# A decoder block on one core: new places for the last gate tiles, two steps of the weight preparation moved, and the start of the attention stage reordered

## The chip, the core and the metric

The kernel runs on one core of a Trainium2 chip. A core has a matrix engine (TensorE, PE in the profile, with its weight loads as PEld), a vector engine (VectorE, DVE), an activation engine (ScalarE, ACT), a general engine (GpSimd, POOL) and an engine that only issues transfers here (SyncE, SP). Each works through its own list of instructions in order and waits on semaphores of the others. Sixteen DMA engines carry the transfers. The metric is the device time of one execution in microseconds (us), the median of several runs.

## The reference

One layer: a wide projection, three groups of dilated sliding-window attention joined by a softmax over the groups' denominators, a gated linear recurrence, two gated merges, an output projection and a layer norm. Sequence 2048, width 1024, 24 heads of 64 (three groups of eight), all float32.

```python
proj = x @ w_in[l] + b_in[l]
q, k, v, g_attn, u_lru, g_lru, gate_logits = jnp.split(proj, SPLIT_POINTS, axis=-1)
q, k = rope(q), rope(k)
for g, (window, dilation) in enumerate(((128, 1), (512, 4), (2048, 16))):
    o_g, lse_g = dilated_band_attention(q[:, :, g], k[:, :, g], v[:, :, g], window, dilation)
wts = softmax(stack(lses));  attn = sum(wts * outs) * silu(g_attn)
y_a = attn @ w_attn_proj[l]
u = causal_depthwise_conv(u_lru, conv_w[l], conv_b[l])
h = rg_lru(u, ...)
y_b = (h * silu(g_lru)) @ w_lru_proj[l]
gates = sigmoid(gate_logits)
out = (gates[0] * y_a + gates[1] * y_b) @ w_out[l] + b_out[l]
x = layer_norm(DEEPNORM_ALPHA * x + out, ln_gain[l], ln_bias[l])
```

## The kernel before

A float32 product is done as three products of rounded parts: each operand is split into a high part (a copy in the format fp32r) and a low part (what is left), and high x high, high x low and low x high are added up in PSUM.

**Stage A, the projection (0 to about 1447 us).** The 72 column tiles of `w_in` are taken in pairs, and the sequence in two halves of two chunks of 512. A pair in a half is a *position*; there are 36 in each half. Except for the first position of each half, a position's 2x2x2 block products are done as seven (Winograd's form of Strassen's method) instead of eight: the weights of a pair are four blocks A11, A12, A21, A22, and the sums are S1 = A21 + A22, S2 = S1 + A11, S3 = A21 + A11 and, here, S4 = S2 + A12. One product is a *tick*: 12 matmuls of 128x512, some 2.7 us. The order of the seven in a position is nearly always MID (1, 6, 7, 5, 2, 4, 3), which uses A11, S2, S3, S1, A12, A22, S4; the last position of a half has EDGE (1, 2, 6, 7, 4, 5, 3), the second position of a half FIRST.

A planner written out in Python sets the order of all engines. It walks through the ticks; at each it writes down the tick's product on PE, then the steps due at that tick (`at(tick, step)`), then steps of longer chains (rotary embedding, the recurrence, stores) as budgets of busy time per engine and free slots allow, and last the step that brings the product out of its PSUM bank (`evacuate`). There are four such banks, so a bank has to be free again four products later. With `t0` four ticks before a position's first product (three in the second half), the position's weights come as follows:

- `load_w` (L225) issues a load of a 128x512 block on SP. In the first half S1 and S3 start as loads of A21 at `t0 - 6`, and GpSimd adds A22 and A11 to them by DMA (`added`, L235) at `t0 - 4`; A11 is loaded at `t0 - 4`, A22 and A12, in that order, at `t0 - 3`. In the second half the low parts come back from DRAM, and A21, A22, A11, A12 are loaded.
- `sums` (L241) at `t0 - 1` forms S2 and then S4 (in the second half S1 before them, and S4 on GpSimd). `sum3` at `t0` forms S3 in the second half.
- `prep_w` (L262) at `t0 + j` splits the j-th block of the order: ScalarE rounds the high part (L266), VectorE takes the low part (helper `tt`, L221).

All tiles of 2 KB a partition in this stage lie in 32 slots; `take` hands out the slot that has been free longest, `give` puts it back. Results of a position are tiles named y. The last two pairs of the sequence are merge gates: each y is put through tanh on ScalarE (L381) and stored into `mg_scr`; from the last position on (`now["n"] >= base[NQ - 1]`), ScalarE issues that store itself (L383).

**Stage B, attention (to about 1665 us).** Its tiles take the same memory as the slots of stage A, and a write waits until the old tile's last reader is done. There are 48 rounds, four for each of 12 units (a group's pair of heads). Round i computes, for four blocks of 128 queries and two heads:

- `scores(i)` on PE into four PSUM banks (tag s); `peak` on VectorE adds the mask and takes the row's extreme (L1007, writes a p tile; eight p tiles rotate); `expo` on ScalarE exponentiates (L1015).
- For round i - 1: `turn` transposes the p tiles on PE into banks of tag t; `bring` copies them to ptb, four copies a round, on ScalarE (L1038) or VectorE (L1040). The third copy goes to VectorE when `light` holds, in every third round and in units of the third group.
- `values(i - 2)` on PE (L1053) into a further bank of tag t, four banks in all for `turn` and `values`; `leave(i - 3)` on VectorE copies that bank out (L1062 and on).

In each round the order is scores(i), leave(i - 3), the exponentials left over, then peaks, transposes, copies and exponentials in turn, and values(i - 2) at the end. Loads of later units and of v go two a round on SP.

**Stage C (to the end)** does the two branch projections, the merge, the output projection and the layer norm, PE being busy throughout.

Of the kernel before, what the change touches and what calls it, by code (L numbers as in the profile page):

```python
# [8 lines left out]
F32 = mybir.dt.float32  # L9
F32R = mybir.dt.float32r  # L10
AF = mybir.ActivationFunctionType
ALU = mybir.AluOpType
# [19 lines left out]
def hybrid_block_kernel(ctx: ExitStack, tc: tile.TileContext, a: dict, out: bass.AP):  # L32
    nc = tc.nc
    sp, act, dve, pool, pe = nc.sync, nc.scalar, nc.vector, nc.gpsimd, nc.tensor
# [56 lines left out]
    now = {"n": 0}  # L91
# [33 lines left out]
    sl_p = stA.enter_context(tc.tile_pool(name="sl_p", bufs=1))  # L125
    ps = stA.enter_context(tc.tile_pool(name="ps", bufs=2, space=PSUM))
    NS, NL = 32, 4
    TRACE = False
    vacant = list(range(NS))
    home = {}  # L130

    def take(name, dt=F32R):
        if not vacant:
            raise RuntimeError(f"no slot at {now['n']}: {[x[1].name if hasattr(x[1],'name') else x[1] for x in home.values()]} chains {len(chains)}")
        i = vacant.pop(0)
        t = sl_p.tile([P, CH], dt, tag=f"s{i}", name=name)
        home[id(t)] = (i, t)
        return t
# [32 lines left out]
    def spend(**eng):  # L171
        for k, v in eng.items():
            if k == "DVE" and now["n"] < base[len(seq)] - 6:
                v *= ALONE
            left[k] = left.get(k, 0.0) - v
# [44 lines left out]
    def tt(eng, out, in0, in1, op):  # L220
        eng.tensor_tensor(out=out, in0=in0, in1=in1, op=op)  # L221


    U, LO, raw = {}, {}, {}

    def load_w(s, n):
        r = raw[s, n] = take(f"w{n}_{s}", F32)
        sp.dma_start(r.rearrange("p (k f) -> p k f", f=P), w_part(s, "A21" if n[0] == "S" else n))

    def w_part(s, n):  # L230

        f = plan[s][1][int(n[1]) - 1][0]
        k = 4 * (int(n[2]) - 1)
        return a["w_in"][f, :, k:k + 4, :]

    def added(s, n, x):

        t = raw[s, n].rearrange("p (k f) -> p k f", f=P)
        pool.dma_start(t, w_part(s, x), accum_op=ALU.add)  # L239

    def sums(s):  # L241
        def add(n, x, y):
            t = raw[s, n] = take(f"{n}_{s}", F32)
            tt(pool if plan[s][0] and n == "S4" else dve, t, raw[s, x], raw[s, y], ALU.add)
        if plan[s][0]:
            add("S1", "A21", "A22")
            spend(DVE=.9)
        add("S2", "S1", "A11")
        add("S4", "S2", "A12")
        if plan[s][0]:  # L250
            spend(DVE=.9, POOL=1.4)
        else:
            spend(DVE=1.45)

    def sum3(s):

        t = raw[s, "S3"] = raw.pop((s, "A21"))
        tt(dve, t, t, raw[s, "A11"], ALU.add)
        spend(DVE=.9)
# [285 lines left out]
    light = [("v", FT_V + 2 * j, FT_V + 2 * j + 1) for j in range(6)]  # L545
# [6 lines left out]
    plan = []  # L552
# [3 lines left out]
    NQ = len(plan)  # L556
    ticks = [8 if pl[2] is None else 7 for pl in plan]
    base = [sum(ticks[:s]) for s in range(NQ + 1)]
# [116 lines left out]
    def at(t, fn):  # L675
        events.setdefault(t, []).append(fn)

    for s in range(1, NQ):
        t0 = base[s] - (3 if plan[s][0] else 4)
        if plan[s][2] is None:  # L680
            for d, n in ((4, "A21"), (4, "A11"), (3, "A22"), (3, "A12")):
                at(t0 - d, lambda s=s, n=n: load_w(s, n))
            for j in range(4):
                at(t0 + j, lambda s=s, j=j: prep_w(s, j))
            continue
        if plan[s][0]:
            for d, n in ((4, "A21"), (4, "A22"), (3, "A11"), (3, "A12")):
                at(t0 - d, lambda s=s, n=n: load_w(s, n))
        else:
            for d, n in ((6, "S1"), (6, "S3"), (4, "A11"), (3, "A22"), (3, "A12")):  # L690
                at(t0 - d, lambda s=s, n=n: load_w(s, n))
            for n, x in (("S1", "A22"), ("S3", "A11")):
                at(max(t0 - 4, 2), lambda s=s, n=n, x=x: added(s, n, x))
        at(max(t0 - 1, 4), lambda s=s: sums(s))
        if plan[s][0]:
            at(t0, lambda s=s: sum3(s))
        for j in range(7):
            if plan[s][0] and j % 2 == 0:
                at(t0 + j - 1, lambda s=s, j=j: load_lo(s, j))
            at(t0 + j, lambda s=s, j=j: prep_w(s, j))  # L700
    for s, pl in enumerate(plan):
        if pl[4] == "ug" and not (pl[0] and pl[1][1][0] - FT_U in put_off):
            at(base[s] + 1, lambda i=pl[1][1][0] - FT_U: fetch_gr(i))
        if pl[0] and pl[4] == "ug":
            i = pl[1][1][0] - FT_U
# [78 lines left out]
    def unit(u):  # L784

        return (0, 2, 1)[u % 3], u // 3
# [135 lines left out]
    for T, (s, j) in enumerate(where):  # L922
# [14 lines left out]
        low = min(low, len(vacant))  # L937
        if TRACE:
            print(T, s, j, plan[s][4], len(vacant), len(lo_vacant), len(chains), {k: round(v, 1) for k, v in left.items()})
    n = len(where)  # L940
# [101 lines left out]
    def values(i):  # L1042
        u, q = divmod(i, 4)
        g, hp = unit(u)
        V = VT[g, hp // 2]
        o = st["o", i] = aps.tile([P, 4, P], F32, tag="t", name=f"o{i}", bufs=4)
        for j in range(4):
            ptb = st["b", i, j // 2]
            n = 4 * q + j
            for x in range(first(i, j) // P, 2):  # L1050
                for h, hs in enumerate(HALF):
                    v0 = P * (hp % 2) + 64 * h
                    pe.matmul(o[hs, j, :], V[:, n if x else prev(g, n), v0:v0 + 64], ptb[:, j % 2, x, h, :],  # L1053
                              start=(x == first(i, j) // P), stop=(x == 1))

    def leave(i):
        u, q = divmod(i, 4)
        g, hp = unit(u)
        o, t = st.pop(("o", i)), ot[u]
        cs = slice(q * CH, (q + 1) * CH)  # L1060
        if g == 0:
            dve.tensor_copy(t[:, cs].rearrange("p (b q) -> p b q", b=4), o)  # L1062
        elif g == 1:
            dve.tensor_copy(t[:, cs].rearrange("p (j r) -> p j r", r=4), o.rearrange("p r j -> p j r"))
        else:
            dve.tensor_copy(t.rearrange("p (j r) -> p j r", r=16)[:, :, 4 * q:4 * q + 4], o.rearrange("p r j -> p j r"))
        if g < 2:
            later(1, lambda: sp.dma_start(o_scr[g][hp][:, cs], t[:, cs]))
        elif q == 3:
            later(1, lambda: sp.dma_start(o_scr[g][hp], t))  # L1070
        if q == 3:
            f0 = 4 * (3 * hp + g)
            dst = st_scr[:, f0:f0 + 4]
            if g == 0:
                later(1, lambda: sp.dma_start(dst.rearrange("(n q) f -> q n f", q=P), sta[u]))
            elif g == 2:
                later(1, lambda: sp.dma_start(dst.rearrange("(q n) f -> q n f", q=P), sta[u]))
            else:
                for c in range(4):
                    later(1, lambda c=c: sp.dma_start(dst[c * CH:(c + 1) * CH].rearrange("(q r) f -> q r f", r=4),  # L1080
                                                      sta[u][:, 4 * c:4 * c + 4]))
# [28 lines left out]
    NG = 48  # L1110
# [4 lines left out]
    for i in range(NG + 3):  # L1115
        u = i // 4
        on, turns = i < NG, 0 < i <= NG
        run(late)
        if i in VORD:
            loads += v_parts(*VORD[i])  # L1120
        if i % 4 == 0 and 1 <= u <= 9:
            loads += unit_parts(u + 2)
        for _ in range(2):
            if loads:
                loads.pop(0)()
        if on:
            scores(i)
        if i > 2:
            leave(i - 3)
        if turns:  # L1130
            expo(i - 1, 2, 1)
            expo(i - 1, 3, 0)
            expo(i - 1, 3, 1)
        if on:
            peak(i, 0, 0)
            expo(i, 0, 0)
            for j, h in ((0, 1), (1, 0), (1, 1)):
                peak(i, j, h)
        if turns:
            turn(i - 1, 0)  # L1140
            bring(i - 1, 0, 0, act)
            bring(i - 1, 0, 1, dve)
        if on:
            for j, h in ((0, 1), (1, 0), (1, 1)):
                expo(i, j, h)
            peak(i, 2, 0)
            peak(i, 2, 1)
        if turns:
            turn(i - 1, 1)
            light = unit((i - 1) // 4)[0] == 2 or i % 3 == 0  # L1150
            bring(i - 1, 1, 0, dve if light else act)
        if on:
            peak(i, 3, 0)
            peak(i, 3, 1)
            expo(i, 2, 0)
        if turns:
            bring(i - 1, 1, 1, dve)
        if i > 1 and i - 2 < NG:
            values(i - 2)
        if i in (40, 41):  # L1160
            prep_wl(i - 40, 2)
        if 42 <= i < 46:
            load_h(0, 2 * (i - 42), 2)
            load_h(0, 2 * (i - 42) + 1, 2)
        if i in (46, 47):
            prep_wl(i - 44, 2)
        now["n"] += 1
# [153 lines left out]
    for n in range(32):  # L1321
        c, f = divmod(n, 8)
# [223 lines left out]
```

## Time and profile before

| | |
|---|---|
| median of 3 runs | 2130.67 us (2128.5, 2130.67, 2130.9) |
| the profiled execution | 2126.78 us, of which the span from first to last instruction 2125.1 us |
| granted TensorE clock, mean over the span | 0.997 |
| DMA | 524.69 MB, mean 247 GB/s |
| chain that ended last, largest lines | PE q L619 43%, ACT p L1015 4%, PE yb L1300 to L1302 3% each |

How to read the rows that follow: a row of a timeline has the start in us, the duration, the engine and line, the operation, what it writes and reads, how many were merged, and in brackets the idle time of the engine before it and what ended that. A "q" behind an engine's name (SPq, ACTq, POOLq) is its sequencer, which issues transfers. A row of the waits has the engine, what it waited for, us in total, how many times, and the longest. Ends of matmuls are modelled.

### The profile page before, as it was taken

To read this page: it belongs to the slowest core of one execution; us is meant where nothing else is said; L and a number is where in the kernel's file an instruction comes from. 1 tells how busy PE (TensorE), PEld (TensorE's weight loads), DVE (VectorE), ACT (ScalarE), POOL (GpSimd) and SP (SyncE) were. 2 spreads that over 40 slices of the span, in tenths; PEclk is the share of its full clock that TensorE was granted. 3 is DMA by queue.
4 is the path that set the end of the run, shared out by engine and by line. 5 is a ranking of instruction groups with operands and counts; after the bars stand their busy time and mean duration, and the time that the engine had idled before them with its cause. 6 is when DMAs were issued, how large, how long until landed. Compare 5 with 4: busy or idle time off the path is not lost.

```text
span 2125.1 us, 35856 instructions
## 1 busy us (share of the span) xinstructions
PE 2084.5 (98%) x12016; PEld 1724.3 (81%) x12016; DVE 1668.6 (79%) x3193; ACT 1124.1 (53%) x2348; POOL 492.1 (23%) x465
## 2 busy tenths in 40 slices
PE   8999999999999999999999999998999999999998
PEld 7888888888888888888887887887888888888887
DVE  8878788899898877787787888776999645576667
ACT  6356455357356565656657666666999411121100
POOL 1111111111111002231131231224435434332120
PEclk9999999999999999999999999999999999999999
DMA  8987997988997976687788788779898788974431
GB/s 276 274 259 228 281 274 215 279 273 243 286 289 229 316 225 194 212 251 208 233 262 267 261 253 257 256 239 391 262 309 255 219 279 285 297 245 155 163 109 70
DMA packets 345832, 524.69 MB, mean 247 GB/s; under 512 B 124208, under 2 KB 153904, under 8 KB 341808
## 3 DMA queue, kind: packets, MB, share of 16 engines
q1 hardware_dynamic: 325760, 489.54, 71.3%
q0 software_dynamic: 12256, 19.42, 5.6%
q10 hardware_dynamic: 7632, 13.44, 1.8%
q8 instruction: 96, 1.57, 0.3%
q14 instruction: 88, 0.72, 0.1%
HBM read 317.14 MB, written 190.45 MB: 239 GB/s over the span
## 4 chain that ended last, share of the span: by engine, by line
PE 68%; ACT 5%; DVE 4%; DMA 2%; issue 1%; SPq 0%; DVEq 0%; ACTq 0%
PE q L619 43%; ACT p L1015 4%; PE yb L1300 3%; PE yb L1301 3%; PE z L1411 3%; PE yb L1302 3%; PE z L1410 3%; PE z L1412 3%; PE o L1053 2%; PE ya L1379 1%; PE ya L1378 1%; PE ya L1380 1%; PE g L489 1%; PE s L1000 1%; ACT ptb L1038 1%
## 5 line engine op out<-in xcount | busy, mean ns | idle before, releaser
L619 PE MATMUL q<-xT,hS 128*128 128x512 f32 x1680 | 520.8, 391 | 0.0
L619 PE MATMUL q<-xT,l 128*128 128x512 f32 x1120 | 436.0, 389 | 0.0
L619 PE MATMUL q<-xB,hA 128*128 128x512 f32 x1248 | 388.3, 392 | 5.6 <-ACT xB L209 5.6
L619 PEld LDWEIGHTS q<-xT,hS 128*128 128x128 f32 x1680 | 313.0, 188 | 69.0 <-issue 5.5
L619 PE MATMUL q<-xB,l 128*128 128x512 f32 x904 | 352.8, 390 | 0.1
L619 PEld LDWEIGHTS q<-xB,hA 128*128 128x128 f32 x1248 | 233.3, 188 | 57.4 <-ACT xB L209 5.6
L619 PEld LDWEIGHTS q<-xT,l 128*128 128x128 f32 x1120 | 210.2, 188 | 44.2
L619 PEld LDWEIGHTS q<-xB,l 128*128 128x128 f32 x904 | 170.0, 188 | 36.6 <-DVE l L221 0.9
L1015 ACT ACTIVATE p<-p,sta 128x256 f32<-128x256 f32 (+1 forms) x384 | 172.1, 455 | 11.7 <-DVE sta L1007 10.9
L239 POOL DMA_DIRECT2D wS<-in_w_in_dram x70 | 61.8, 955 | 502.9 <-DMA wS<-in_w_in_dram 117.3
L619 PE MATMUL q<-xB,hS 128*128 128x512 f32 x560 | 174.2, 392 | 2.4 <-DVE v L221 2.4
L619 PE MATMUL q<-xT,hA 128*128 128x512 f32 x560 | 173.0, 390 | 0.1
L266 ACT ACTIVATE hA<-wA 128x512 fp32r<-128x512 f32 x218 | 135.1, 624 | 64.3 <-DMA wA<-in_w_in_dram 25.9
L266 ACT ACTIVATE hS<-S 128x512 fp32r<-128x512 f32 x175 | 109.0, 623 | 85.0 <-DVE S L221 46.6
L221 POOL TENSOR_TENSOR S<-S,wA 128x512 f32<-128x512 f32 x35 | 45.5, 1300 | 423.1 <-DVE S L221 256.3
L1007 DVE CUSTOM_DVE_ANT_0 p<-s,mask 128x256 f32<-128x256 f32 (+1 forms) x384 | 118.9, 360 | 11.6 <-DMA mg_scr<-y 7.2
L619 PEld LDWEIGHTS q<-xB,hS 128*128 128x128 f32 x560 | 103.8, 188 | 25.4 <-issue 4.6
L619 PEld LDWEIGHTS q<-xT,hA 128*128 128x128 f32 x560 | 104.7, 188 | 23.4 <-issue 2.0
L221 DVE TENSOR_TENSOR l<-wA,hA 128x512 fp32r<-128x512 f32 x113 | 79.4, 703 | 27.8 <-ACT hA L266 27.6
L1411 PE MATMUL z<-wo,mh 128*128 128x512 f32 (+1 forms) x264 | 101.0, 383 | 0.0
L1412 PE MATMUL z<-wo,ml 128*128 128x512 f32 (+1 forms) x264 | 101.0, 383 | 0.0
L1410 PE MATMUL z<-wo,mh 128*128 128x512 f32 (+1 forms) x264 | 101.0, 383 | 0.0
(201 smaller groups left out, 4234.6 us busy)
## 6 DMA issues: line engine op xcount, KB each, us to landing
wA<-in_w_in_dram SPq DMA_DIRECT2D x253, 256.0 KB, 4.8
wl_scr<-l SPq DMA_DIRECT2D x105, 512.0 KB, 4.8
l<-wl_scr SPq DMA_DIRECT2D x105, 512.0 KB, 4.6
sw<-y SPq DMA_DIRECT2D x384, 64.0 KB, 3.2
wS<-in_w_in_dram SPq DMA_DIRECT2D x70, 256.0 KB, 4.8
wS<-in_w_in_dram POOLq DMA_DIRECT2D x70, 256.0 KB, 6.1
qh_scr<-hi SPq DMA_DIRECT2D x48, 256.0 KB, 5.4
v_scr<-vs SPq DMA_DIRECT2D x48, 256.0 KB, 4.5
```

Of the source, the lines that this page charges most:

```text
L221: eng.tensor_tensor(out=out, in0=in0, in1=in1, op=op)
L239: pool.dma_start(t, w_part(s, x), accum_op=ALU.add)
L266: act.activation(h, r, AF.Copy)
L619: pe.matmul(bank, w[:, ks], x[:, kk, xx], start=(first and i == 0), stop=(last and i == 11))
L1007: dve.tensor_tensor_reduce(out=st["p", i, j][:, h, lo:256], in0=st["s", i, j // 2][h][:, j % 2, lo:256], in1=mask[:, lo:256], scale=1.0, s ...
L1015: act.activation(p, p, AF.Exp, scale=-1.0, bias=s[:, h:h + 1], accum_out=s[:, 2 + h:3 + h])
L1300: pe.matmul(yb, WL[f][:, 0, k], xx[:, 0], start=(k == 0), stop=False)
L1301: pe.matmul(yb, WL[f][:, 0, k], xx[:, 1], start=False, stop=False)
L1302: pe.matmul(yb, WL[f][:, 1, k], xx[:, 0], start=False, stop=(k == 7))
L1410: pe.matmul(z, mh[:, k], w[:, 0, hs], start=(k == 0), stop=False)
L1411: pe.matmul(z, mh[:, k], w[:, 1, hs], start=False, stop=False)
L1412: pe.matmul(z, ml[:, k], w[:, 0, hs], start=False, stop=(k == 7))
```

## The change

Four parts. The last position's y tiles are put into chosen slots (31, 7, 8, 9, 30 as long as they are free) instead of the one free longest. S4 is formed by a step of its own, a tick later than S2. In the first half A12 is loaded ahead of A22, and A22 at a tick that depends on where product 4 stands in the order: a tick behind `t0` in MID instead of three ticks ahead of it, at `t0` in EDGE. At the start of stage B, values(0) comes behind scores(3), its copy-out `leave(0)` at the end of round 3, and the third copy of rounds 1 and 2 goes to VectorE.

```diff
+    LATE = [31, 7, 8, 9, 30]
...
     def take(name, dt=F32R):
...
-        i = vacant.pop(0)
+        i = vacant[0]
+        if name[0] == "y" and now["n"] >= base[NQ - 1]:
+            i = next((x for x in LATE if x in vacant), i)
+            if i in LATE:
+                LATE.remove(i)
+        vacant.remove(i)
...
+    def add_w(s, n, x, y):
+        t = raw[s, n] = take(f"{n}_{s}", F32)
+        on_pool = plan[s][0] and n == "S4"
+        tt(pool if on_pool else dve, t, raw[s, x], raw[s, y], ALU.add)
+        spend(**({"POOL": 1.4} if on_pool else {"DVE": .9 if plan[s][0] else .72}))
+
     def sums(s):
-        def add(n, x, y):
-            t = raw[s, n] = take(f"{n}_{s}", F32)
-            tt(pool if plan[s][0] and n == "S4" else dve, t, raw[s, x], raw[s, y], ALU.add)
         if plan[s][0]:
-            add("S1", "A21", "A22")
-            spend(DVE=.9)
-        add("S2", "S1", "A11")
-        add("S4", "S2", "A12")
-        if plan[s][0]:
-            spend(DVE=.9, POOL=1.4)
-        else:
-            spend(DVE=1.45)
+            add_w(s, "S1", "A21", "A22")
+        add_w(s, "S2", "S1", "A11")
...
-            for d, n in ((6, "S1"), (6, "S3"), (4, "A11"), (3, "A22"), (3, "A12")):
+            d22 = 3 if s == 1 else 4 - plan[s][2].index(4)
+            for d, n in ((6, "S1"), (6, "S3"), (4, "A11"), (3, "A12"), (d22, "A22")):
                 at(t0 - d, lambda s=s, n=n: load_w(s, n))
...
         at(max(t0 - 1, 4), lambda s=s: sums(s))
+        at(max(t0, 4), lambda s=s: add_w(s, "S4", "S2", "A12"))
...
         if on:
             scores(i)
-        if i > 2:
+        if i == 3:
+            values(0)
+        if i > 3:
             leave(i - 3)
...
-            light = unit((i - 1) // 4)[0] == 2 or i % 3 == 0
+            light = unit((i - 1) // 4)[0] == 2 or i < 3 or i % 3 == 0
             bring(i - 1, 1, 0, dve if light else act)
...
-        if i > 1 and i - 2 < NG:
+        if i > 2 and i - 2 < NG:
             values(i - 2)
+        if i == 3:
+            leave(0)
```

What this makes of the engines' lists is shown at three places; the changed kernel's line numbers are some lines higher (L227 for L221, L1012 for L1007, L1005 for L1000, L1030 for L1025, L1058 for L1053).

VectorE in the first half, between positions 20 and 21 (the two S rows are S2 and S4 of position 21, v is the step that brings out the third product of position 20), before and then after:

```order
L221 TENSOR_TENSOR S_21_4340<-wS_21_4205,wA_21_4259 128x512
L221 TENSOR_TENSOR S_21_4342<-S_21_4340,wA_21_4289 128x512
L221 TENSOR_TENSOR gw_0_4344<-gr_201,gw_0_4344 128x128
L221 TENSOR_TENSOR v_4348<-u_4321,q_20_4323 128x512
L221 TENSOR_TENSOR l_21_4365<-wA_21_4259,hA_21_4363 128x512
```

```order
L227 TENSOR_TENSOR S_21_4338<-wS_21_4205,wA_21_4259 128x512
L227 TENSOR_TENSOR gw_0_4340<-gr_201,gw_0_4340 128x128
L227 TENSOR_TENSOR v_4344<-u_4319,q_20_4321 128x512
L227 TENSOR_TENSOR S_21_4359<-S_21_4338,wA_21_4287 128x512
L227 TENSOR_TENSOR l_21_4363<-wA_21_4259,hA_21_4361 128x512
```

S4 moved behind gw and v; the low part of A11 still follows it.

VectorE where stage A ends and stage B begins (the last y tile, then the masking writes into p tiles, each with a row that reads out its accumulator), with what each waits for; DMAHW is a counter of landed transfers. Before and then after:

```order
L221 TENSOR_TENSOR y_3_14420<-q_71_14401,u_14330 128x512 [waits DVE_49,PE_49]
L1007 ISA p_14483,sta_14453<-s_14455,mask 128x128 [waits PE_49]
L1007 ISA sta_14453 128x1
L1007 ISA p_14483,sta_14453<-s_14456,mask 128x128 [waits PE_49]
L1007 ISA sta_14453 128x1
L1007 ISA p_14487,sta_14453<-s_14455,mask 128x256 [waits DMAHW5_49,Activation_49]
```

```order
L227 TENSOR_TENSOR y_3_14420<-q_71_14401,u_14330 128x512 [waits DVE_49,PE_49]
L1012 ISA p_14483,sta_14453<-s_14455,mask 128x128 [waits PE_49]
L1012 ISA sta_14453 128x1
L1012 ISA p_14483,sta_14453<-s_14456,mask 128x128 [waits PE_49]
L1012 ISA sta_14453 128x1
L1012 ISA p_14487,sta_14453<-s_14455,mask 128x256 [waits DMAHW7_49]
```

The order is the same; the third write waited for the store of the last y tile (y63_3) before, and now for that of an older one (y62_3).

PE in rounds 2 and 3 (s are scores of round 3, o the values of round 0, pt transposes), before and then after:

```order
L1025 MATMUL pt_14664<-ident,p_14592 128x64
L1025 MATMUL pt_14665<-ident,p_14592 128x64
L1053 MATMUL o_14689<-ptb_14563,V_14369 64x128 x6
L1053 MATMUL o_14689<-ptb_14590,V_14369 64x128 x8
L1000 MATMUL s_14704<-B_14303,A_14327 128x256
```

```order
L1005 MATMUL s_14704<-B_14303,A_14327 128x256
L1058 MATMUL o_14717<-ptb_14563,V_14369 64x128 x6
L1058 MATMUL o_14717<-ptb_14590,V_14369 64x128 x8
L1030 MATMUL pt_14742<-ident,p_14630 128x64
L1030 MATMUL pt_14743<-ident,p_14630 128x64
```

The values of round 0 stood ahead of the scores of round 3 and now stand between them and the transposes of round 2.

## The prediction, made before the changed kernel had run

> **What bounds the kernel now.** I read the page's busy times first, then the waits of PE, then busy times by stage, then the places where PE waits.
>
> ```profile
> PE 2084.5 (98%) x12016; PEld 1724.3 (81%) x12016; DVE 1668.6 (79%) x3193; ACT 1124.1 (53%) x2348; POOL 492.1 (23%) x465
> PE o L1053 <- ACT ptb L1038: 14.3, 43, 0.6
> PE s L1000 <- DVE sta L1007: 7.4, 1, 7.4
> PE q L619 <- DVE v L221: 2.4, 2, 1.6
> ```
>
> PE is idle for 40.6 of 2125.1 us, so no reordering can bring more than 2%. The waits say where: one of 7.4 us at the first scores, 43 small ones in the attention stage, and two that come to 2.4 us in the projection stage. Busy time by stage (time, then PE, PEld, DVE, ACT, POOL busy with counts, granted clock, DMA share, GB/s):
>
> ```profile
> 1400.00:1446.50 46.50, 46.50 (x207) 38.50 (x206) 30.34 (x43) 28.72 (x44) 7.44 (x7) 1.00 0.85 289
> 1452.00:1456.00 4.00, 0.00 (x0) 0.00 (x0) 0.00 (x0) 0.00 (x0) 1.39 (x2) 0.59 1.04 424
> 1456.00:1461.00 5.00, 4.18 (x46) 4.10 (x48) 3.76 (x21) 3.79 (x15) 0.00 (x0) 0.50 1.00 406
> 1461.00:1470.00 9.00, 8.12 (x140) 7.48 (x138) 8.04 (x34) 9.00 (x35) 3.16 (x4) 0.89 1.03 416
> ```
>
> Up to 1446.5 PE alone is the bound. Then PE, VectorE and ScalarE are all empty from 1452 to 1456, and right after that ScalarE is full (9.00 of 9.00) while VectorE has about one us to spare. A us won before 1446 or in the empty stretch moves all that follows; in the full stretch only less work on ScalarE helps, as far as VectorE can take it.
>
> **The handover, second by second.**
>
> ```profile
> 1447.70 0.72 ACT L381 ACTIVATE y<-y,bh 128x512 f32<-128x512 f32 x1 [2.00 <-DVE y L221]
> 1447.72 1.67 PE L1000 MATMUL s<-B,A 64*128 64x128 f32 x23 [0.53 <-DVE y L221]
> 1448.46 0.33 ACTq L383 DMA_DIRECT2D mg_scr<-y  x1
> 1448.61 0.29 DVE L1007 CUSTOM_DVE_ANT_0 p<-s,mask 128x128 f32<-128x128 f32 x1 [0.94 <-PE s L1000]
> 1448.82 0.29 DVE L1007 CUSTOM_DVE_ANT_0 p<-s,mask 128x128 f32<-128x128 f32 x1
> 1456.33 0.42 DVE L1007 CUSTOM_DVE_ANT_0 p<-s,mask 128x256 f32<-128x256 f32 x1 [7.21 <-DMA mg_scr<-y]
> 1456.68 0.42 DVE L1007 CUSTOM_DVE_ANT_0 p<-s,mask 128x256 f32<-128x256 f32 x1
> 1456.82 3.37 PE L1000 MATMUL s<-B,A 64*128 64x256 f32 x24 [7.42 <-DVE sta L1007]
> 1456.85 0.51 ACT L1015 ACTIVATE p<-p,sta 128x256 f32<-128x256 f32 x1 [7.03 <-DVE sta L1007]
> 1460.77 0.49 ACT L1038 ACTIVATE ptb<-pt 128x384 f32<-128x384 f32 x1 [0.36 <-PE pt L1025]
> 1467.88 1.69 PE L1000 MATMUL s<-B,A 64*128 64x256 f32 x24
> ```
>
> The last gate tile is stored from 1448.46, on DMA engines that are full (share 1.04). VectorE's third masking write goes into the bytes that this store still reads, so it waits 7.21 us; PE and ScalarE wait for VectorE. In the changed kernel that tile (y63_3) lies at byte 149184 of the partition instead of 132800. That write goes to the second p tile, 134592 to 136640, which the old place overlapped; the new place is under a tile first written in round 7 (rounds count from 0). Without the wait the third write follows as the second did the first (0.21 after it): at 1449.03, **7.30** earlier. PE's second scores start 0.49 later, at 1449.52, 0.13 after its first ones end (1447.72 + 1.67 = 1449.39); ScalarE goes on where it stopped, at 1449.82, **7.03** earlier.
>
> What is late next at that place: the same p tile now waits for the store of an older gate tile, y62_3.
>
> ```profile
> 1429.48 0.33 ACTq L383 DMA_DIRECT2D mg_scr<-y  x1
> ```
>
> With 7.74 us, as long as the last one took (1448.46 to 1456.2), it is over by 1437.3. And PE's clock: the granted clock falls to 0.50 about 3.3 us after PE stopped (0.59 is the mean of 1452 to 1456), and the scores at 1456.82 take 3.37 us for what takes 1.69 at 1467.88. ScalarE lost 0.36 us to the slow PE (row 1460.77); I count these **0.36** as won, since the gap shrinks to 0.13.
>
> [...]
>
> **Copies from ScalarE to VectorE, and the values a round later.** In rounds 1 and 2 one copy each changes engine. The first three rows are from the chain of waits, where a row is the time that its work holds the chain; the others are PE's timeline.
>
> ```profile
> 1467.62 0.48 ACT ptb L1038
> 1468.10 2.46 ACT p L1015 x10
> 1509.32 0.60 DVE ptb L1040
> 1466.20 1.75 PE L1053 MATMUL o<-ptb,V 128*64 128x128 f32 x28 [0.57 <-ACT ptb L1038]
> 1469.41 1.15 PE L1025 MATMUL pt<-ident,p 64*128 64x64 f32 x32
> 1471.10 1.97 PE L1053 MATMUL o<-ptb,V 128*64 128x128 f32 x32 [0.54 <-ACT ptb L1038]
> ```
>
> ScalarE loses 2 x 0.48 = **0.96**; five exponentials hold it 2.46, so a round of eight and one copy is 4.4 instead of 4.9. VectorE gains 2 x 0.60 = 1.20: eight masking writes at 0.35 (1456.33 to 1456.68) and three copies make 4.6. ScalarE alone would thus come to the end of round 3 earlier by 7.03 + 0.36 + 0.96 = **8.35**.
>
> But the moved values bring PE work into round 3. There PE does scores (1.5 to 1.69), the values of round 0 (1.75), the transposes, and the values of round 1 (1.97). Before, the 1.75 lay in round 2 and held up the scores of 1467.88. Counted on from 1449.03: VectorE ends the masking of round 2 after 22 more writes (7.7) and five copies (3.0), at 1459.7. Then come the other half of the scores (0.8) to 1460.5, values to 1462.25, half the transposes (0.55), a copy (0.60; with values of round 0 not yet copied out, the transposes have three of the four PSUM banks and wait for that copy) and the other half (0.6). So the values that started at 1471.10 start at 1464.0, **7.1** earlier. From there PE's work leads the chain of waits, so I take **7.5**, near the PE count and below ScalarE's. Copying out round 0's values (0.69 on VectorE) goes to the end of round 3, where VectorE waits for PE's values anyway. Bounds: 8.35 above; below, 7.1 less all that VectorE newly does in these rounds, 1.20 and 0.69, so 5.2.
>
> **Projection stage.** The two waits on DVE v:
>
> ```profile
> 427.81 0.70 PE L619 MATMUL q<-xB,hS 128*128 128x512 f32 x2 [0.76 <-DVE v L221]
> 585.39 0.70 PE L619 MATMUL q<-xB,hS 128*128 128x512 f32 x2 [1.65 <-DVE v L221]
> 421.41 0.91 SPq L228 DMA_DIRECT2D wA<-in_w_in_dram  x2
> 426.17 0.69 DVE L221 TENSOR_TENSOR S<-S,wA 128x512 f32<-128x512 f32 x1 [5.06 <-issue]
> 426.98 0.68 DVE L221 TENSOR_TENSOR v<-u,q 128x512 f32<-128x512 f32 x1
> 583.75 0.69 DVE L221 TENSOR_TENSOR S<-S,wA 128x512 f32<-128x512 f32 x1 [4.34 <-DMA wA<-in_w_in_dram]
> ```
>
> The sum S4 = S2 + A12 stood for 5.06 and 4.34 us before its weights had landed (A22 and A12 issue at 421.41, A12 second); v, which frees a bank for PE, was behind it. Now v is ahead of S4 and A12 ahead of A22, so S4's wait blocks nothing that is due within a product. I count both as gone: 0.76 + 1.65 = **2.41**. Below: two new stalls of the longest size, 2.41 - 3.30 = -0.9. In the second half S4 is on GpSimd, which passes one other instruction in three places; nothing there.
>
> A22's load now goes out four products later (three in the last position), with the next position's loads:
>
> ```profile
> 424.49 0.94 SPq L228 DMA_DIRECT2D wS<-in_w_in_dram  x1
> 438.66 0.62 ACT L266 ACTIVATE hA<-wA 128x512 fp32r<-128x512 f32 x1
> wA<-in_w_in_dram SPq DMA_DIRECT2D x253, 256.0 KB, 4.8
> ```
>
> It stands right before the wS load that went out at 424.49, at the very position that stalled, and ScalarE rounds A22 at 438.66. Landing takes 4.8 at the median, so 9.4 us are left over. I price it at nothing. Behind it on SP wait the two wS loads, one issue (0.45) later.
>
> **Sum.** 2.41 + 7.5 = 9.9 us. The profiled execution took 2126.78 (span 2125.1 and 1.7 around it), so 2116.9 by its own time; from the median of 2130.67, **2120.8**. That execution lies 3.9 under the median; I keep this as scatter in the range.
>
> **Rivals.**
>
> *Only part at the handover.* VectorE leads from round 1 on, and its 1.89 us of new work all lies on the path, or a stall returns in the projections: 5.2 - 0.9 to 7 us won, 2123.7 to 2126.4. For it speaks VectorE's 8.04 of 9.00, against it the us that it waits there. Chance 0.13.
>
> *DMA takes over.* Loads do not come sooner, as the DMA engines are full. The first that could hurt is ql of unit 1:
>
> ```profile
> 1449.40 0.33 SPq L821 DMA_DIRECT2D A<-ql_scr  x1
> SPq L821 <- DMA A<-ql_scr: 1.7, 1, 1.7
> 1459.45 0.32 SPq L821 DMA_DIRECT2D A<-ql_scr  x1
> 1473.00 1.56 PE L1000 MATMUL s<-B,A 64*128 64x128 f32 x24
> ```
>
> The next ql issue waits for that landing, so it was in by 1459.45; PE needs it at 1473.00 - 7.5 = 1465.5. If 6 us more of it were late, the win would fall to about 4: 2127. Chance 0.03.
>
> *The wait stays* (some other store under an early p tile): only 2.41 won, 2128.3. The addresses speak against it. Chance 0.05.
>
> *Slower: A22 lands late.* ScalarE works in order, so from the point where A22's issue lags more than 9.4 us it stands, and the copies and weights behind it come late. Of the 34 positions, every third losing the longest stall seen, 11 x 1.65 = 18.2, gives 2130.67 - 9.9 + 18.2 = 2139. SP's loads did go out late by several us at 421.41. Chance 0.04.
>
> *VectorE blocked by GpSimd's S4*, since in the second half S3 on VectorE is issued in the same product as S4 now. One S3 already took 1521 ns:
>
> ```profile
> L221 DVE TENSOR_TENSOR wA<-wA,wA x35: 683/797/1521, 743.6 to 1421.0; 128x512 f32<-128x512 f32 x35
> ```
>
> All 35 from 797 to 1521 is 25 us of VectorE; at 30.34 busy of 46.50 it has room, and PE would see it only if it fell four products behind. A tenth reaching PE is 2.5: 2123.3, chance 0.03. [...]
>
> **Numbers.** Forecast (gains of 8 to 11): 0.72. The others: 0.13, 0.03, 0.05, 0.04, 0.03. A measurement here tells 0.2%, 4.3 us, from no change. Faster by more: 0.72 + 0.13 + 0.03, and half of DMA's, 0.89; within: 0.07; slower: 0.04. Range: 8.35 + 2.41 = 10.8 under the median is 2119.9, and 3.9 for executions that lie as the profiled one does, 2116; above 5.2 - 0.9 = 4.3, 2126.4.
>
> **What would show it.** VectorE's wait on mg_scr and PE's 7.4 us gone, granted clock 1.00 across the handover; the two q waits on v gone; ScalarE full until round 3, values of round 1 some 7.5 us after the shift of stage A earlier. I am wrong if ScalarE waits for wA where A22 is rounded, if VectorE's idle before L1012 reappears under another name, or if the end of the attention stage has moved by less than the handover.

## The result, and the profile after

The changed kernel takes **2120.03 us** (median of 6 runs, 2118.86 to 2121.78). The kernel before takes 2129.06 us (median of 6 runs, 2126.51 to 2130.90; three of the six are those shown at the start). The ratio is 0.9958, with a 95% interval of 0.9946 to 0.9971: 9.0 us faster. The profiled execution of the changed kernel took 2119.04 us, with a span of 2117.3.

First the page's busy times and a selection of the waits of PE (engine and line, what it waited for, us in total, times, longest us):

```profile
PE 2084.1 (98%) x12016; PEld 1723.0 (81%) x12016; DVE 1666.3 (79%) x3195; ACT 1122.6 (53%) x2346; POOL 490.7 (23%) x465
PE o L1058 <- ACT ptb L1043: 13.0, 41, 0.6
PE s L1005 <- DVE sta L1012: 2.2, 3, 1.1
PE pt L1030 <- ACT ptb L1043: 0.6, 1, 0.6
PE ya L1388 <- DVE at L1097: 0.5, 1, 0.5
PE q L622 <- DVE y L227: 0.4, 1, 0.4
PE z L1421 <- DVE ml L1406: 0.3, 1, 0.3
```

PE's busy time is the same to 0.4 us, so all that was won is idle time. The wait of 7.4 us at the scores and the two on v are gone. Three shorter waits on `sta` (2.2), one on a copy (0.6), one on a y tile in the projections (0.4), and two in stage C (0.5 and 0.3) are new.

Then busy time around the handover (time, PE, PEld, DVE, ACT, POOL with counts, granted clock, DMA share, GB/s):

```profile
1446.50:1461.00 14.50, 12.04 (x190) 10.01 (x186) 13.00 (x63) 13.14 (x53) 3.92 (x5) 1.00 1.04 399
```

```profile
1446.50:1461.00 14.50, 6.55 (x72) 5.77 (x73) 4.96 (x26) 5.40 (x20) 6.73 (x7) 0.71 1.05 400
```

The first row is after, the second before. VectorE and ScalarE go from 5 of 14.5 us to 13, and the granted clock is full (1.00, against 0.71).

Last, the timelines there, VectorE's masking writes and then PE:

```profile
1446.65 0.28 DVE L1012 CUSTOM_DVE_ANT_0 p<-s,mask 128x128 f32<-128x128 f32 x1
1446.87 0.42 DVE L1012 CUSTOM_DVE_ANT_0 p<-s,mask 128x256 f32<-128x256 f32 x1
```

```profile
1444.70 0.32 PE L1005 MATMUL s<-B,A 64*128 64x128 f32 x1
1447.44 2.60 PE L1005 MATMUL s<-B,A 64*128 64x256 f32 x24 [0.21 <-DVE sta L1012]
1457.24 1.32 PE L1005 MATMUL s<-B,A 64*128 64x256 f32 x12 [1.11 <-DVE sta L1012]
1458.49 1.75 PE L1058 MATMUL o<-ptb,V 128*64 128x128 f32 x28
1461.57 0.70 PE L1030 MATMUL pt<-ident,p 64*128 64x64 f32 x15 [0.63 <-ACT ptb L1043]
1462.20 1.97 PE L1058 MATMUL o<-ptb,V 128*64 128x128 f32 x32
1464.10 1.56 PE L1005 MATMUL s<-B,A 64*128 64x128 f32 x24
```

The third masking write follows 0.22 behind the second. Rounds count from 0: the rows show the scores of round 0 (1444.70, its first product), of round 1 (1447.44), half of round 3 (1457.24), the moved values of round 0 (1458.49), and the scores of round 4 (1464.10). Such starts are the marks for all that follows.

Where the 7.74 us between the two spans (2125.07 and 2117.33) came from:

| stretch | before, us | after, us | difference |
|---|---|---|---|
| start to scores of round 0 | 1446.87 | 1444.70 | -2.17 |
| scores of round 0 to round 1 | 9.95 | 2.74 | -7.21 |
| scores of round 1 to round 4 | 16.18 | 16.66 | **+0.48** |
| scores of round 4 to the end of the last values | 194.72 | 194.53 | -0.19 |
| end of the last values to the end | 457.35 | 458.70 | +1.35 |

So the wait itself brought 7.21 us, and the three rounds behind it, where the reordering is, take longer than before, although before they ran partly at half the clock (0.50 until 1462.94).

### The profile page after: what moved, and what is told of

It reads as the page before. It is cut to its first block, busy times and chain, and to the rows that moved or that the text cites. A ratio compares the mean times of both kernels' runs of the same rounds, so it can differ in the third digit from the quotient of the medians.

```text
span 2117.3 us, 35897 instructions
## 1 busy us (share of the span) xinstructions
PE 2084.1 (98%) x12016; PEld 1723.0 (81%) x12016; DVE 1666.3 (79%) x3195; ACT 1122.6 (53%) x2346; POOL 490.7 (23%) x465
## 4 chain that ended last, share of the span: by engine, by line
PE 85%; ACT 5%; DVE 4%; DMA 4%; issue 1%; SPq 1%; POOL 0%; DVEq 0%; ACTq 0%
PE q L622 62%; ACT p L1020 4%; PE z L1419 2%; PE z L1421 2%; PE z L1420 2%; PE yb L1309 2%; PE yb L1311 2%; PE yb L1310 2%; PE o L1058 2%; PE g L492 1%; DVE p L1012 1%; PE s L1005 1%; PE ya L1388 1%; ACT ptb L1043 1%; PE ya L1389 1%
## 5 line engine op out<-in xcount | busy, mean ns | idle before, releaser
L269 ACT ACTIVATE hA<-wA 128x512 fp32r<-128x512 f32 x218 | 135.0, 623 | 60.0 <-DMA wA<-in_w_in_dram 24.5
L227 POOL TENSOR_TENSOR S<-S,wA 128x512 f32<-128x512 f32 x35 | 45.5, 1300 | 393.6 <-DVE S L227 225.2
L1012 DVE CUSTOM_DVE_ANT_0 p<-s,mask 128x256 f32<-128x256 f32 (+1 forms) x384 | 118.9, 360 | 3.9 <-PE s L1005 3.0
L1309 PE MATMUL yb<-h,wl 128*128 128x512 f32 x256 | 100.3, 392 | 0.0
```

Source lines behind the costliest of these rows:

```text
L269: act.activation(h, r, AF.Copy)
L1012: dve.tensor_tensor_reduce(out=st["p", i, j][:, h, lo:256], in0=st["s", i, j // 2][h][:, j % 2, lo:256], in1=mask[:, lo:256], scale=1.0, s ...
L1309: pe.matmul(yb, WL[f][:, 0, k], xx[:, 0], start=(k == 0), stop=False)
```

## The experiments

Each is one profiled execution, unless a median is given. For all of them the same three stretches are read off PE's timeline; *handover* is from the scores of round 0 to those of round 4.

| run | time, us | scores of round 0 at | round 0 to 1 | round 1 to 4 | handover |
|---|---|---|---|---|---|
| before | 2126.78 | 1446.87 | 9.95 | 16.18 | 26.13 |
| after | 2119.04 | 1444.70 | 2.74 | 16.66 | 19.40 |
| e1 slots alone | 2119.68 | 1447.23 | 2.74 | 15.78 | 18.52 |
| e2 weights alone | 2117.35 | 1444.28 | 2.73 | 15.80 | 18.53 |
| e3 attention alone | 2127.18 | 1445.80 | 9.81 | 17.69 | 27.50 |
| e6 slots and weights | 2118.45 | 1444.15 | 2.74 | 17.02 | 19.76 |
| e4 after, values back | 2115.57 | 1443.43 | 2.74 | 14.95 | 17.69 |
| e5 after, copies back | 2118.00 | 1443.84 | 2.74 | 16.42 | 19.16 |
| e7 S4 alone | 2120.81 | 1444.55 | 2.74 | 19.15 | 21.89 |
| e10 weights, old slot | 2125.45 | 1444.53 | 9.79 | 16.18 | 25.97 |
| e9 PE kept busy | 2128.32 | 1447.30 | 9.86 | 16.91 | 26.77 |
| e11 bank sooner | 2118.64 | 1444.81 | 2.74 | 16.65 | 19.39 |

The time of one execution says little here: the kernel before alone took 2126.31 to 2130.90 in the runs beside these. The stretches say more: where two kernels have the same order from round 1 to round 4 and the clock is full, they agree within 0.02 us (15.78 and 15.80; 16.66 twice; 14.95 twice).

### The parts alone

Slots alone:

```diff
+    LATE = [31, 7, 8, 9, 30]
...
+        if name[0] == "y" and now["n"] >= base[NQ - 1]:
+            i = next((x for x in LATE if x in vacant), i)
...
```

> The kernel before with only the new slots for the last gate tiles. If the overlap of the last y tile with the second p tile was the whole 7.2 us wait (my theory), VectorE's wait on mg_scr is gone, the granted clock stays 1.00 across the handover, the projections keep both waits (0.76 and 1.65 us, last product at 1446.9), and the scores of round 4 stand about 7.0 + 0.36 = 7.4 us earlier than the 1473.00 of before, since ScalarE is full from round 0 on. If the reordering of the attention start is needed to use the gap (rival), the scores of round 4 gain clearly less than the 6.73 us that the full change gained at the handover, 5 to 6 us.

Weights (S4 and A22) alone:

```diff
-        add("S4", "S2", "A12")
...
-            for d, n in ((6, "S1"), (6, "S3"), (4, "A11"), (3, "A22"), (3, "A12")):
+            d22 = 3 if s == 1 else 4 - plan[s][2].index(4)
+            for d, n in ((6, "S1"), (6, "S3"), (4, "A11"), (3, "A12"), (d22, "A22")):
...
+        at(max(t0, 4), lambda s=s: add_w(s, "S4", "S2", "A12"))
...
```

> The kernel before with only S4 a tick later, A12 ahead of A22 and A22 later. My theory: PE's last projection product ends 2.2 to 2.4 us earlier than 1446.94 (the two waits on DVE v gone), the handover keeps its wait of about 7.2 us and the half clock, the end is 2.2 to 2.4 us earlier. Rival (the gain in the full change came from the other planner state, that is from the slots): under 1 us.

Attention alone (values of round 0 moved, copies of rounds 1 and 2 on VectorE):

```diff
+        if i == 3:
+            values(0)
...
-            light = unit((i - 1) // 4)[0] == 2 or i % 3 == 0
+            light = unit((i - 1) // 4)[0] == 2 or i < 3 or i % 3 == 0
...
```

> The kernel before with only the values of round 0 behind the scores of round 3 and the third copy of rounds 1 and 2 on VectorE; the wait at the handover stays. If ScalarE bounds rounds 1 to 3 there (my theory) the scores of round 4 come 0.5 to 1.0 us earlier than 1473.00. If VectorE takes over as the bound (rival, as the full change's trace hints: 13.00 of 14.5 us busy), they move by less than 0.3 us either way or come later.

Slots and weights without the attention part (the first two diffs together):

> The full change without its reordering of the attention start (values of round 0 where they were, third copy of rounds 1 and 2 on ScalarE). If the parts add up (my theory) the projections end about 2.2 us earlier and the handover brings what the slots alone bring; against the full change's 1464.10 for the scores of round 4 this is 0 to 0.7 us earlier if ScalarE alone was the bound before, and 0.5 to 1 us later if the reordering helps.

Slots alone shorten the handover by 26.13 - 18.52 = 7.61, more than the whole change did (6.73); the theory of that run held. Attention alone made it 1.37 longer (27.50): the theory there, a gain of 0.5 to 1.0, failed, and the scores of round 4 came at 1473.30, later than the 1473.00 of before, as the rival had it. Slots and weights together came out at 19.76 because of the clock, told below.

Weights alone were a surprise: the wait at the handover was gone there too. The planner hands out the slot that has been free longest, so moving two steps of the weights moves every later tile; with them alone the last gate tile, y63_3, falls at byte 143040 instead of 132800, under a tile of output that is written later. (The bytes are those that the programs give to these tiles.) The expectation that the wait would stay was wrong. Two theories were left: the place, or something in the earlier weights.

### The place of the last gate tile

S4 and A22 moved as in the change, and that one tile forced back to byte 132800:

```diff
-        i = vacant.pop(0)
+        i = 1 if name == "y63_3" and 1 in vacant else vacant[0]
+        vacant.remove(i)
```

> S4 and A22 as in the changed kernel, attention as before, and the last gate tile alone forced into the slot that it had before (byte 132800, under the second p tile). With S4 and A22 alone it had fallen elsewhere (143040) and the handover wait was gone. If only the place counts (theory): VectorE's third masking write waits 7.2 us for mg_scr<-y again, the granted clock falls to 0.50, the end comes 7 to 8 us later than with S4 and A22 alone, so a span of 2123 to 2124, while the projection stage keeps its 2.5 us. If the earlier end of the weights' sums took the wait away (rival): span 2115.6 to 2116.5.

Only S4 a tick later, A22 as before; here the planner puts y63_3 under the first ptb tile:

```diff
-        add("S4", "S2", "A12")
...
+        at(max(t0, 4), lambda s=s: add_w(s, "S4", "S2", "A12"))
```

> Only S4 a product later; A22, slots and attention as before. The two waits of PE's q on v in the projections (2.4 us) go if S4 is their cause; if A22's place ahead of A12 also matters, one of 0.5 to 1.7 stays. The last gate tile (y63_3) now falls under the first transposed tile (ptb of heads 0 and 0) that ScalarE copies in round 0. If the handover wait is a matter of the tile under which the last store reads (theory), VectorE's third masking write waits for nothing, and instead the first copy ptb<-pt on ScalarE waits for mg_scr<-y for some 3 to 5 us, till about 8 us after that store was issued. If the wait goes with anything else in the change (rival), it is either 7.2 us at VectorE's third masking write or gone without a new wait.

The third masking write with the old slot; then, with S4 alone, the store, the third masking write and the first copies to ptb:

```profile
1453.83 0.42 DVE L1007 CUSTOM_DVE_ANT_0 p<-s,mask 128x256 f32<-128x256 f32 x1 [7.05 <-issue]
```

```profile
1446.13 0.33 ACTq L380 DMA_DIRECT2D mg_scr<-y  x1
1446.71 0.42 DVE L1005 CUSTOM_DVE_ANT_0 p<-s,mask 128x256 f32<-128x256 f32 x1
1454.09 0.49 ACT L1036 ACTIVATE ptb<-pt 128x384 f32<-128x384 f32 x1 [3.15 <-DMA mg_scr<-y]
1454.13 0.56 DVE L1038 COPY ptb<-pt 128x384 f32<-128x384 f32 x1 [3.89 <-DMA mg_scr<-y]
```

With the old slot the wait is back (7.05 us, ended 7.7 after the store's issue at 1446.12; the row puts no name to what ended it, but it is the wait of before in place and length), and the handover is 25.97, near the 26.13 of before, while the projections kept their gain. With the tile under ptb, VectorE's third write waits for nothing, and the same store, issued at 1446.13, holds ScalarE and VectorE instead, until 8.0 us later. So the tile that lies under the last store decides who waits, and nothing else in the change does.

S4 alone also answers for the projections: the scores of round 0 start 2.32 earlier, and PE no longer waits for v, but once for another low part (vl) that now stands behind S4 (waits of PE from 100 to 1440 us):

```profile
PE g L486 <- DVE vl L221: 1.0, 1, 1.0
```

VectorE still waits for A12's load in S4, 9.2 us in two waits between 415 and 600 us. With A12 loaded first as well, the changed kernel's VectorE waits 5.5 there, in two. A22's part in the projections lies below what one execution can show; A22 alone was not run.

### The two halves of the attention part

The changed kernel with the values of round 0 back in round 2:

```diff
-        if i == 3:
-            values(0)
-        if i > 3:
+        if i > 2:
             leave(i - 3)
...
-        if i > 2 and i - 2 < NG:
+        if i > 1 and i - 2 < NG:
             values(i - 2)
-        if i == 3:
-            leave(0)
```

> The changed kernel with the values of round 0 back in round 2, the copies still on VectorE. From the scores of round 1 to those of round 4 it was 15.78 and 15.80 us with neither attention edit, 16.66 in the changed kernel. If the moved values are what costs (theory): 15.8 or less, down to 14.9 if the two copies of 0.48 taken off ScalarE all count. If the copies on VectorE are what costs (rival): 16.4 to 16.7. If neither does by itself: 15.8.

The changed kernel with the copies back on ScalarE:

```diff
-            light = unit((i - 1) // 4)[0] == 2 or i < 3 or i % 3 == 0
+            light = unit((i - 1) // 4)[0] == 2 or i % 3 == 0
```

> The changed kernel with the two copies back on ScalarE, the values of round 0 still moved to round 3. From the scores of round 1 to those of round 4, if the moved values cost (theory): 16.7 or more, up to 17.6 with the two copies back on ScalarE. If the copies on VectorE cost (rival): 15.8.

From round 1 to round 4: 15.8 with neither, 14.95 with the copies alone, 16.42 with the moved values alone, 16.66 with both. The copies bring 0.84 where the values stay, and cost 0.24 (16.42 to 16.66) where they are moved; the moved values cost 0.63 by themselves and 1.71 with the copies. For the moved values alone neither expectation held: 16.42 is under the one and over the other, because the two edits interact. With the copies on ScalarE, ScalarE is full all through these rounds with the moved values too (12.00 of 12.00 us from 1450 to 1462), which lets part of PE's added work hide behind it. First the changed kernel without the moved values, its busy time and PE's rows of the values of round 0 and the scores of round 3; then two rows of waiting in the changed kernel with them:

```profile
1446.50:1461.00 14.50, 12.67 (x224) 11.23 (x223) 14.43 (x62) 14.49 (x57) 3.17 (x4) 1.00 1.03 408
1454.68 1.75 PE L1058 MATMUL o<-ptb,V 128*64 128x128 f32 x28 [0.57 <-ACT ptb L1043]
1456.36 1.70 PE L1005 MATMUL s<-B,A 64*128 64x256 f32 x24
```

```profile
1460.92 0.60 ACT L1043 ACTIVATE ptb<-pt 128x512 f32<-128x512 f32 x1 [1.09 <-PE pt L1030]
1460.95 0.69 DVE L1045 COPY ptb<-pt 128x512 f32<-128x512 f32 x1 [1.44 <-PE pt L1030]
```

Without the moved values VectorE and ScalarE are both full (14.43 and 14.49 of 14.50). With them both stand for 1.44 and 1.09 us at 1460.9, waiting for transposes that PE has behind the 1.75 us of moved values at 1458.49. In round 2 the same values run at 1454.68 while both engines have work in store, and the scores of round 3 then follow without a wait, whereas in the changed kernel PE first stands 1.11 us for VectorE's masking (row 1457.24) and runs the values after that, when the other two are about to run dry.

The moved values also hold a bank of PSUM for longer. To see what that costs, `leave(0)` was put in the middle of round 3:

```diff
             bring(i - 1, 0, 1, dve)
+            if i == 3:
+                leave(0)
...
-        if i == 3:
-            leave(0)
```

> The changed kernel, with the values of round 0 copied out of their PSUM bank by VectorE in the middle of round 3 rather than at its end, while VectorE is idle anyway. From the scores of round 1 to those of round 4 the changed kernel takes 16.66 us, without the moved values 14.95. If the moved values cost because PE runs their 1.75 us ahead of the transposes for which VectorE and ScalarE stand (theory): 16.0 to 16.7, the 0.63 us wait for a bank gone at most. If they cost because they hold a PSUM bank (rival): 15.0 to 15.4.

It took 16.65, as if nothing had been changed: VectorE reached the copy-out only at 1461.66, behind the copy that stood till 1461.06, and PE's wait of 0.63 stayed. So the bank was not free sooner, and this run does not separate the two, though 16.65 lies in the range of the theory; but all that PE waits for a bank is 0.63, so the bank can be at most that part of 1.71. That the rest comes from the place of the values on PE is read from the rows above.

### The clock

The kernel before, with work of no use on PE during the wait:

```diff
+        if i == 0:
+            busy = aps.tile([P, CH], F32, tag="t", name="busy", bufs=4)
+            for _ in range(28):
+                pe.matmul(busy, units[0][1][:, 0, 0:P], units[0][1][:, 0, 0:CH], start=True, stop=True)
```

> The kernel before, with 28 added 128x512 products of no use to the output issued on PE between the scores of round 0 and those of round 1, so that PE works through most of the handover wait, which stays. If idle PE is what halves the clock (theory): granted clock 1.00 throughout, scores of round 1 in 2.6 us in place of 3.37, ScalarE's wait of 0.36 for the transposes gone, and from the scores of round 1 to those of round 4 15.8 us, where the kernel before took 16.18. If the clock falls with the change of stage (rival): 0.50 there as before, and 16.2.

```profile
1449.75 6.64 PE L1131 MATMUL busy<-B 128*128 128x512 f32 x28
1457.16 2.70 PE L1000 MATMUL s<-B,A 64*128 64x256 f32 x24 [0.77 <-DVE sta L1007]
1466.07 2.58 PE L1053 MATMUL o<-ptb,V 128*64 128x128 f32 x28 [0.57 <-ACT ptb L1038]
1468.58 2.42 PE L1000 MATMUL s<-B,A 64*128 64x256 f32 x24
```

VectorE waited 7.1 us for the store as before, the change of stage was the same, and the clock stayed at 1.00 through the wait, where it had been 0.50, and until 1466.8: the scores of round 1 took 2.70, not 3.37, and ScalarE's wait of 0.36 was gone. So PE's idling, and not the change of stage, is what halved the clock in that wait. But the expectation of 1.00 throughout and of 15.8 us to round 4 was missed (16.91), since the clock fell later: values that take 1.75 at full clock took 2.58. The same happened with slots and weights together. One-microsecond windows there:

```profile
1453.00:1454.00 1.00, 0.71 (x15) 0.44 (x12) 1.00 (x7) 1.00 (x5) 0.00 (x0) 1.00 1.02 418
1454.00:1455.00 1.00, 0.69 (x10) 0.41 (x12) 1.00 (x4) 1.00 (x5) 0.00 (x0) 1.00 0.98 389
1455.00:1456.00 1.00, 0.43 (x8) 0.29 (x10) 1.00 (x7) 1.00 (x4) 0.00 (x0) 1.00 0.97 393
1456.00:1457.00 1.00, 1.00 (x14) 1.00 (x16) 0.39 (x1) 1.00 (x5) 0.00 (x0) 0.62 1.02 410
1457.00:1458.00 1.00, 1.00 (x14) 1.00 (x12) 0.00 (x0) 1.00 (x4) 0.00 (x0) 0.50 1.06 422
1459.00:1460.00 1.00, 1.00 (x14) 1.00 (x16) 0.55 (x1) 0.75 (x4) 0.00 (x0) 0.67 1.02 406
```

A mean of 0.62 over 1456 to 1457 puts the fall at 1456.24 (0.24 at 1.00, the rest at 0.50); 0.67 over 1459 to 1460 puts the return at 1459.66, so 3.42 us. PE was not idle before it, only thinly busy: 0.71, 0.69 and 0.43 of the three whole microseconds ahead.

### The version without the moved values, timed

The changed kernel again and the version of e4, five rounds each beside the kernel before (2128.72 us, median of 9, 2126.41 to 2130.34):

> The changed kernel once more, for the comparison with the version without the moved values: 2120 us, ratio to before 0.995 to 0.997.

> The changed kernel without the moved values (slots, S4, A22 and the copies on VectorE stay), timed. If the trace's 1.71 us between the scores of rounds 1 and 4 reach the end (theory): 1.2 to 2.2 us below the changed kernel's median. If later stages take them back (rival): within 0.5 us of it.

The changed kernel took 2118.66 (2116.70 to 2123.12), ratio 0.9955 (0.9941 to 0.9968). The version without the moved values took 2117.87 (2115.91 to 2119.06), ratio 0.9948 (0.9936 to 0.9961). Both are faster than before; the 0.8 us between them is not told apart by these runs. Their profiled executions repeat the stretch from round 1 to round 4, 16.66 and 14.95. The two expectations on the end are both missed: 0.8 lies between them. What varies is stage C. From the last values to the end it took 457.35 before, 458.70 in the changed kernel's first profile, and in these two 460.81 and 460.57. The waits of PE in stage C in the changed kernel's second profile:

```profile
PE ya L1387 <- DVE gA L1392: 1.7, 1, 1.7
PE z L1421 <- DVE ml L1406: 0.8, 1, 0.8
```

VectorE waits there for gate tiles coming back from DRAM (gA from mg_scr), 0.9 us in the kernel before between 1840 and 1900, 7.6 in this execution. It is not the earlier end of attention that costs: slots alone, whose attention ended 7.15 earlier, lost nothing (457.33), and the old slot, 2.68 earlier, lost 1.36. Nor is it all scatter. The nine profiled executions in which S4 and A22 are both moved take 457.9 to 460.8 us in stage C (mean 458.8); the five others, S4 alone among them, take 457.3 to 457.7 (mean 457.5). So the longer stage C goes with A22's move, and gives back 1.3 us on average. Whether A22's later load does it, or the other order that the planner then makes, and by what wait, is open: VectorE's waits for gA alone do not decide it, being 9.7 us in the run with the earlier copy-out, where stage C took 457.9.

## Why the prediction was right, step by step

It said 2120.8 us, in a range of 2116.0 to 2126.4; measured were 2120.03. Against its own base it was a little high: 9.9 us were to be won, 9.0 were, and the median of before, over six runs in place of three, stood 1.6 lower. That the forecast lies only 0.8 off is in part luck: 1.6 too high a start and 0.9 too much gain work against each other. The main causes, the slot and S4, were right; the term for the attention part was not.

**The wait at the handover: right.** From the scores of round 0 to VectorE's third masking write it was 1456.33 - 1446.87 = 9.46, and is 1446.87 - 1444.70 = 2.17: 7.29 less, where 7.30 was said. The slot under the store was the cause (old slot, S4 alone), and nothing took its place at that point: the store of y62_3 held no one.

**The clock, 0.36: right in size and cause at this place.** With the old slot and in the kernel before, rounds 1 to 4 take 16.18; with the slot free and the attention order as before, 15.78 and 15.80. The gap that was put at 0.13 us is 0.21 in the changed kernel (row 1447.44), and the granted clock is 1.00 from 1446.5 to 1461. But that the clock stays full once the long gap is gone does not always hold: with slots and weights together it fell to 0.50 later in the same rounds, though PE had no gap over 0.57 us there, and the stretch took 17.02.

**Copies to VectorE, 0.96 for ScalarE: right only without the moved values.** There they bring 0.84, and ScalarE's count of 8.35 for slots, clock and copies came out at 26.13 - 17.69 = 8.44. In the changed kernel itself they cost 0.24.

**Moved values: the step that was mis-sized.** The count on PE was close: counted on, the values of round 1 start 7.1 earlier than before. They started at 1462.20, and with the projections' 2.17 put back, at 1464.37 where the count said 1464.0; the handover won 6.73. But the prediction then took 7.5, between PE's 7.1 and ScalarE's 8.35. Here the two engines, which wait for each other, did not share the difference: the later one set the time. By its own count the term should have been 7.1, still 0.4 above what was measured. The prediction did not ask either what the handover would win without that edit. It is 7.61 with the slots alone and 8.44 with the copies as well, so the moved values took 1.71 back, and the attention part as a whole cost 0.88 (18.52 to 19.40); that they would stand ahead of the transposes in round 3 was in its own count. Its sign that ScalarE is full until round 3 did not come: ScalarE stood for 1.09 us there.

**Projections, 2.41: right for the stage.** The profile of after shows 2.17, with one new wait of 0.4 for a y tile. In the nine profiled executions with S4 and A22 both moved, the scores of round 0 start 1.92 to 3.44 earlier (mean 2.53); in the three without either (slots alone, attention alone, PE kept busy) 0.36 and 0.43 later and 1.07 earlier. A22's later load was priced at nothing, and in the rounding nothing was late: ScalarE waited 24.5 us for wA there, 25.9 before. But stage C is longer in every execution with A22 moved, so at the end the weights bring, on average, some 1.3 us less than in the stage.

**DMA behind it.** The first transfer in danger was sought in attention, and there nothing was late: from round 4 to the last values the time is the same to 0.2. What was given back, 1.35 here, was given back in stage C, which the prediction had not looked at. Of the rivals, only part of the handover won came nearest in kind, since 6.73 of 7.5 were won there; but its 4.3 to 7 was for the whole gain, which was 9.0, and VectorE's new work did not all lie on the path: the copies cost 0.24 of their 1.20. Nor did GpSimd's S4 hold VectorE up more than before: the 35 S3 of the second half took 804 ns at the median and 1195 at most, against 797 and 1521 before.

## What to carry to other kernels

When two engines wait for each other and their counts of a stretch differ, start from the later one, not from a value between. Before crediting work that is moved out of a full stretch, look at who is fed by what it now stands ahead of: here 1.75 us of PE work was harmless while VectorE and ScalarE had work in store, and cost 1.71 one round later. When a planner hands out memory, any edit to the order moves every later tile, so a wait on reuse can come and go with edits that have nothing to do with it; compare addresses before naming a cause.

## What the hardware showed that was not expected

In three of these runs the stretches at a granted clock of 0.50 were 3.42, 6.84 and 10.24 us long, the longer two 2.00 and 2.99 times the shortest, and ahead of the shortest PE had no gap over 0.57 us in these rounds. The clock was 0.50 for 3.42 us with slots and weights together, and in the kernel before for 10.24 (0.85 over 1452 to 1453 puts the fall at 1452.70; 0.53 over 1462 to 1463 the return at 1462.94). With S4 alone it was 6.84, read in the same way (0.85 over 1453 to 1454, 0.73 over 1460 to 1461). In as long a time, 3.42 us, ahead of the fall at 1456.24, PE was busy for 2.25 (0.71, 0.69 and 0.43 in the three whole windows, and all of the 0.18 ahead of them and the 0.24 behind), 66%. With PE kept busy the later fall, at 1466.82, also came behind 3.42 us of which PE was busy for 2.33, 68%. Busy is what the profile shows, with modelled ends of matmuls. With weights alone the order in these rounds is the same, and the gaps too, and the clock did not fall:

```profile
1454.00:1455.00 1.00, 0.68 (x8) 0.40 (x8) 1.00 (x4) 1.00 (x5) 0.00 (x0) 1.00 0.98 352
1455.00:1456.00 1.00, 0.40 (x6) 0.26 (x6) 1.00 (x7) 1.00 (x4) 0.00 (x0) 1.00 0.90 320
1456.00:1457.00 1.00, 0.99 (x18) 0.99 (x20) 0.51 (x1) 1.00 (x5) 0.00 (x0) 1.00 1.02 418
```

What decides between the two was not shown. The stretch at 0.50 goes with 17.02 - 15.80 = 1.2 us in the one execution, and in the other there was none.
